# Issue order at the start, five accumulator banks in the output projection, and moved weight tiles in a two-layer attention kernel

## The chip, the cores and the metric

The kernel runs on one core of a Trainium2 chip (trn2). The metric is the device time of one execution in microseconds (us), lower is better; the time given for a kernel is the median of its runs. The core has five engines that work side by side and are tied together by semaphores: TensorE (PE, matmul), VectorE (DVE), ScalarE (ACT), GpSimd (POOL) and SyncE (SP, which here only issues transfers).

## The reference

Two layers work on a stream x of 1024 tokens by 1024 features, with 256 memory tokens beside it. All is float32.

```
layer 0:  u = rms_norm(x) * g ; p = u @ w_in      (7168 columns)
          8 heads of differential attention (two softmax maps each, position bias, q and k normalised)
          a gated causal convolution of width 3 over 512 channels
          4 heads of attention to the memory tokens
          h = x + concat(each branch * silu(its gate)) @ w_out
layer 1:  the same frame, with 12 heads of "forgetting" attention (a cumulative
          log-sigmoid bias per head) and 4 heads of attention to the memory tokens
out = h
```

## The kernel before

**Precision.** A float32 matmul is made from float32r parts: every operand is split into a high part (a ScalarE copy, L128) and the rest (a subtraction on VectorE or GpSimd, L129), and each product is three matmuls: high by high, high by low, low by high. The helper is `split` (L125). Weights come through raw buffers in SBUF (tag "raw", four of them) and are split into `wqh`/`wql` (eight tiles each, tags of the pool `pw`) or, for gate and convolution columns, into `wfh`/`wfl`.

**Start.** `run` (L810) opens two pools for layer 0, `p1_0` and then `pw_0`, takes the norm weights `gb` and goes over eight blocks of 128 tokens. For each it loads x (tag "E1", three buffers) on the SP queue, squares it on ScalarE (L135), gets the reciprocal root on GpSimd (L120, L122), scales on VectorE (L137), transposes on TensorE (L146) and splits the result into `u`, the moving or stationary operand of all projections. Ahead of the third block it asks for the weights of the first head's q, k and v columns: `unit_weights` (L167) makes eight tiles of 384 columns, each from three transfers of 64 KB, with the low parts alternately on VectorE and GpSimd. Behind the blocks come `params` (L64: small transfers of per-feature gains, some with a small product on VectorE) and `lam_setup` (L478: a transfer, three VectorE steps and an exponential on ScalarE). Then `diff_head(0)` runs the unit: `token_unit` (L187), eight blocks of 24 matmuls with 384 columns. While `boot` is set the unit takes accumulator banks from the tags "d" and "s" in turn. After the first head's gate columns, the function `first` (L830) does the memory branch of both layers: `mem_norm` and `mem_kv`.

**PSUM.** Of eight banks, tag "d" has three (projections), "s" two (attention scores), "t" two (transposes) and "o" one (attention outputs).

**Output projection.** `out_proj` (L763) opens a pool `p2` when the layer's `p1` and `pw` are closed; the pools share addresses, and a tile waits for those that it overlies (`reuse_waits="tile"`). In `p2` lie 32 tiles `wo` of 2 KB per partition for the second half of the output columns (first the 16 high parts, then the 16 low parts), `gb2` and four tiles `hb`. The first half of the columns goes over token blocks in pairs: `out_blocks` (L737) takes one "d" bank for each block, and over four groups of four chunks loads y back (ACT queue), splits it into `yh`/`yl` (three buffers each) and runs 12 matmuls per block and group. When a pair is done, VectorE adds the residual in `hb` (L782) and frees the banks. The second half goes block by block and, in layer 0, normalises each finished block for layer 1 (L805).

**Layer 1.** `run` opens `p1_1` and then `pw_1` where `p2_0` was. `fox_head(0)` (L669) runs a unit of 396 columns (12 more for the forget gates), with the low weight parts all on GpSimd.

**Order.** The kernel's text does not fix the order of the queues. The framework plans it with a simulated clock: among the instructions that are ready it takes the one with the highest priority, which is the place in the text unless a block raises it (`high_priority` by 4000 or 8000 places). Each engine then works through its queue strictly in that order.

Of the kernel before, what the change touches and what calls it, by code (L numbers as in the profile page):

```python
# [7 lines left out]
F32 = mybir.dt.float32  # L8
F32R = mybir.dt.float32r
# [6 lines left out]
P = 128  # L16
T = 1024
D = 1024
# [8 lines left out]
PRIO_EVAC, PRIO_ATT = 8000, 4000  # L27
# [6 lines left out]
class Trunk:  # L34
# [26 lines left out]
        self.attb, self.gorder = 3, (3, 2, 1, 0)  # L61
        self.wq_n, self.e1b, self.ptb = 384, 3, 2

    def params(self):  # L64
        nc, io = self.nc, self.io

        def col(name, src, n, reps=1):
            t = self.const.tile([P, 1], F32, name=name)
            for r in range(reps):
                nc.sync.dma_start(out=t[r * n:(r + 1) * n, :], in_=src.rearrange("a n -> n a"))  # L70
            return t

        def prod(name, a, b, s):
            t = self.const.tile([P, 1], F32, name=name)
            nc.vector.tensor_tensor(out=t, in0=a, in1=b, op=ALU.mult)
            nc.vector.tensor_scalar(out=t, in0=t, scalar1=s, scalar2=None, op0=ALU.mult)
            return t

        self.g_a = prod("g_a", col("aq", io["e_a_q_norm_g"], 64, 2), col("ak", io["e_a_k_norm_g"], 64, 2), 64.0 ** -0.5)
        self.g_c = prod("g_c", col("cq", io["o_c_q_norm_g"], P), col("ck", io["o_c_k_norm_g"], P), float(P) ** -0.5)  # L80
        self.g_x = [
            prod("g_x0", col("xq0", io["e_x_q_norm_g"], P), col("xk0", io["e_x_k_norm_g"], P), float(P) ** -0.5),
            prod("g_x1", col("xq1", io["o_x_q_norm_g"], P), col("xk1", io["o_x_k_norm_g"], P), float(P) ** -0.5),
        ]
        og = col("og", io["e_a_out_norm_g"], P)
        self.g_o = self.const.tile([P, 1], F32, name="g_o")
        nc.vector.tensor_scalar(out=self.g_o, in0=og, scalar1=0.5 * (1.0 - LAM_INIT), scalar2=None, op0=ALU.mult)

        self.lam = self.const.tile([P, 1], F32, name="lam")
        self.cw = self.const.tile([P, 4, 3], F32, name="cw")  # L90
        for k in range(3):
            nc.sync.dma_start(out=self.cw[:, :, k], in_=io["e_b_conv_w"][0, k].rearrange("(g p) -> p g", p=P))
        self.cb = self.const.tile([P, 4], F32, name="cb")
        nc.sync.dma_start(out=self.cb, in_=io["e_b_conv_b"][0].rearrange("(g p) -> p g", p=P))
        self.fb = self.const.tile([P, 12], F32, name="fb")
        nc.sync.dma_start(out=self.fb, in_=io["o_c_forget_b"].broadcast_to([P, 12]))
# [357 lines left out]
    def qkv_unit(self, w, cols, ng, gs, g, extra=None, pairs=False, weights=None):  # L454
        nc = self.nc
        qh, ql, kh, kl, vh, vl = self.att_tiles("qh", "ql", "kh", "kl", "vh", "vl")
        kd, kz = self.att_tiles("kd", "kz") if pairs else (None, None)
        qns = []

        def post(tb, ps):  # L460
            raw = self.evac(ps, 384 if extra is None else 396)
            qns.append(self.qk_norm(raw, ng, gs))
            vs = slice(tb % 4 * P, (tb % 4 + 1) * P)
            self.split(vh[tb // 4][:, vs], vl[tb // 4][:, vs], raw[:, 256:384], nc.gpsimd)
            if extra is not None:
                extra[1](tb, raw)
            if tb % 2:
                if pairs:
                    self.later(DEFER, lambda: self.qk_transpose_pairs(qns[tb - 1:tb + 1], (qh, ql), (kh, kd, kl, kz), g, (tb - 1) * P))
                else:  # L470
                    self.later(DEFER, lambda: self.qk_transpose(qns[tb - 1:tb + 1], [(qh, ql, g), (kh, kl, None)], (tb - 1) * P))
        if weights is None:
            weights = self.unit_weights(w, [(c, P) for c in cols] + ([] if extra is None else [extra[0]]))
        self.token_unit(weights, self.u_lhs(0), self.u_lhs(1), NB, post)
        return (qh, ql), (kh, kd, kl, kz) if pairs else (kh, kl), *[(lambda kb, v=v: v[kb // 4][:, kb % 4 * P:(kb % 4 + 1) * P]) for v in (vh, vl)]

# [260 lines left out]
    def out_blocks(self, layer, tbs, tiles, fetch=None):  # L737

        nc = self.nc
        pss = [self.bank("pd", "d") for _ in tbs]  # L740
        for j in range(4):
            if fetch is not None:
                fetch(range(4 * j, 4 * j + 4))
            for tb, ps in zip(tbs, pss):
                ts = slice(tb * P, (tb + 1) * P)
                yr = self.pk.tile([P, 4, P], F32, name="yr2", tag="yr", bufs=4)
                nc.scalar.dma_start(out=yr, in_=self.y_dr[layer][tb // 2][j][tb % 2])
                if layer == 0 and j < 2:
                    rn = self.pa.tile([P, 4, P], F32, name="rn", tag="hs", bufs=3)
                    nc.scalar.dma_start(out=rn, in_=self.on_dr[j][tb].unsqueeze(0).broadcast_to([P, 4, P]))  # L750
                    nc.gpsimd.tensor_tensor(out=yr, in0=yr, in1=rn, op=ALU.mult)
                yh = self.pa.tile([P, 4, P], F32R, name="yh2", tag="wfh", bufs=3)
                yl = self.pa.tile([P, 4, P], F32R, name="yl2", tag="wfl", bufs=3)
                self.split(yh, yl, yr, nc.vector)
                for i in range(4):
                    c = 4 * j + i
                    h, l = tiles(0, c), tiles(1, c)
                    nc.tensor.matmul(ps, lhsT=yh[:, i, :], rhs=h, start=(c == 0), stop=False)  # L758
                    nc.tensor.matmul(ps, lhsT=yh[:, i, :], rhs=l, start=False, stop=False)  # L759
                    self.last_mm = nc.tensor.matmul(ps, lhsT=yl[:, i, :], rhs=h, start=False, stop=(c == 15))  # L760
        return pss

    def out_proj(self, layer, w, res, dst, g_next):  # L763
        nc, tc = self.nc, self.tc
        with tc.tile_pool(name=f"p2_{layer}", bufs=1, reuse_waits="tile") as p2:
# [2 lines left out]
            u, early = self.u, self.early  # L768
            ne = len(early[0])
            w0 = lambda part, c: early[part][c] if c < ne else u[part][(c - ne) // 8][:, (c - ne) % 8, :]  # L770
            ws = [[p2.tile([P, 512], F32R, name=f"wo{p}_{c}") for c in range(16)] for p in range(2)]
            w1 = lambda part, c: ws[part][c]

            gb = p2.tile([P, D], F32, name="gb2")
            hbs = [p2.tile([P, D], F32, name=f"hb{i}") for i in range(4)]
# [34 lines left out]
    def run(self, out):  # L810
        nc, tc, io = self.nc, self.tc, self.io
        mem = io["mem"][0]
        with tc.tile_pool(name="p1_0", bufs=1, reuse_waits="tile") as self.p1, tc.tile_pool(name="pw_0", bufs=1, reuse_waits="tile") as self.pw:
            gb = self.pk.tile([P, T], F32, name="gb", tag="bias", bufs=1)
            self.new_u()
            w, weights = io["e_w_in"][0], None
            for tb in range(NB):
                if tb == 2:
                    weights = self.unit_weights(w, [(c, P) for c in self.diff_cols(0)], (nc.vector, nc.gpsimd))
                with tc.high_priority(PRIO_EVAC):  # L820
                    xn = self.p1.tile([P, T], F32, name="xn", tag="E2", bufs=2)
                    x = self.p1.tile([P, T], F32, name="x", tag="E1", bufs=self.e1b)
                    nc.sync.dma_start(out=x[:, :D], in_=io["x"][0, tb * P:(tb + 1) * P, :])
                    if tb == 0:
                        nc.sync.dma_start(out=gb, in_=io["e_norm_g"].broadcast_to([P, D]))
                    self.norm_block(x[:, :D], gb, xn[:, :D], *self.u_dst(tb))
            self.params()
            self.lam_setup()

            def first():  # L830
                kv = self.mem_kv(0, self.mem_norm(0, mem, io["e_mem_norm_g"]), io["e_w_mem_kv"][0])
                for _ in range(2):
                    next(kv)
                kv1 = self.mem_kv(1, self.mem_norm(1, mem, io["o_mem_norm_g"]), io["o_w_mem_kv"][0])
                for _ in (*kv, *kv1):
                    pass
                self.bias = self.pk.tile([P, T], F32, name="abias", tag="bias", bufs=1)
                nc.gpsimd.iota(self.bias, pattern=[[1, T]], base=-(NB - 1) * P, channel_multiplier=-1, allow_small_or_imprecise_dtypes=True)
                nc.gpsimd.affine_select(out=self.bias, in_=self.bias, pattern=[[-1, T]], compare_op=ALU.is_ge, fill=NEG,
                                        base=(NB - 1) * P, channel_multiplier=1)  # L840
# [5 lines left out]
            for pr in range(2):  # L846
                self.x_pair(0, pr, w, 6144, 6656, io["e_w_out"][0])
        self.out_proj(0, io["e_w_out"][0], io["x"][0], self.h_dr, io["o_norm_g"])
        with tc.tile_pool(name="p1_1", bufs=1, reuse_waits="tile") as self.p1, tc.tile_pool(name="pw_1", bufs=1, reuse_waits="tile") as self.pw:
            self.wq_n, self.e1b, self.ptb = 396, 3, 3  # L850
            w = io["o_w_in"][0]
            self.cqn = self.p1.tile([P, NB, 12], F32, name="cqn")
# [36 lines left out]
```

## Time and profile before

| what | value |
|---|---|
| median of three runs | 2222.51 us (2221.56 to 2222.58) |
| the profiled execution | 2226.73 us, its span 2224.9 us |
| TensorE busy | 2177.0 us, 98% of the span |
| VectorE, ScalarE, GpSimd busy | 1251.2, 1057.3 and 1025.4 us |
| moved by transfers | 183.05 MB, mean 82 GB/s |

Times in the rows are microseconds from the start of the span, unless ns is marked. PE is TensorE, PEld its weight load, DVE VectorE, ACT ScalarE, POOL GpSimd, SPq and ACTq the queues that issue transfers. In a timeline row the bracket says how long the engine was idle before the instruction and what ended that. PEclk is the granted clock of TensorE as a share of 2.4 GHz; 0.50 is 1.2 GHz. Matmuls overlap, so the distance from start to start, not the duration, is what one costs.

### The profile page before, as it was taken

To read this page: it belongs to the slowest core of one execution; us is meant where nothing else is said; L and a number is where in the kernel's file an instruction comes from. 1 tells how busy PE (TensorE), PEld (TensorE's weight loads), DVE (VectorE), ACT (ScalarE), POOL (GpSimd) and SP (SyncE) were. 2 spreads that over 40 slices of the span, in tenths; PEclk is the share of its full clock that TensorE was granted. 3 is DMA by queue.
4 is the path that set the end of the run, shared out by engine and by line. 5 is a ranking of instruction groups with operands and counts; after the bars stand their busy time and mean duration, and the time that the engine had idled before them with its cause. 6 is when DMAs were issued, how large, how long until landed. Compare 5 with 4: busy or idle time off the path is not lost.

```text
span 2224.9 us, 35832 instructions
## 1 busy us (share of the span) xinstructions
PE 2177.0 (98%) x12528; PEld 1975.1 (89%) x12528; DVE 1251.2 (56%) x2860; ACT 1057.3 (48%) x2503; POOL 1025.4 (46%) x1356
## 2 busy tenths in 40 slices
PE   7999999999999999999989999999999999999999
PEld 6889889899898899777879999999999999998787
DVE  5646656665665667653525555555555555666432
ACT  5655465464554555432334444444444444554321
POOL 4565555555555453342335555544555555431200
PEclk9999999999999999999999999999999999999999
DMA  5350210201202112486522222211222221123643
GB/s 164 123 158 23 65 52 19 72 28 52 62 26 59 36 53 89 127 269 190 182 60 49 58 58 58 58 35 47 46 55 67 58 62 43 47 70 121 220 130 103
DMA packets 222108, 183.05 MB, mean 82 GB/s; under 512 B 24636, under 2 KB 179420, under 8 KB 221928
## 3 DMA queue, kind: packets, MB, share of 16 engines
q1 hardware_dynamic: 198888, 138.82, 21.8%
q10 hardware_dynamic: 23040, 41.95, 6.2%
q8 instruction: 98, 1.61, 0.3%
q14 instruction: 82, 0.67, 0.1%
HBM read 153.32 MB, written 27.38 MB: 81 GB/s over the span
## 4 chain that ended last, share of the span: by engine, by line
PE 91%; DMA 4%; DVE 1%; ACT 1%; POOL 1%; issue 1%; SPq 1%; ACTq 0%; POOLq 0%; DVEq 0%
PE pd L199 11%; PE pd L200 11%; PE pd L198 11%; PE pss L391 8%; PE pd L232 7%; PE pd L231 7%; PE pd L233 7%; PE pd L758 5%; PE pd L760 5%; PE pd L759 5%; PE pt L425 4%; PE po L439 2%; PE po L440 2%; PE po L438 2%; PE pt L280 1%
## 5 line engine op out<-in xcount | busy, mean ns | idle before, releaser
L198 PE MATMUL pd<-wqh,u 128*128 128x384 f32 (+2 forms) x1536 | 515.7, 337 | 3.3 <-ACT wqh L128 2.4
L199 PE MATMUL pd<-wql,u 128*128 128x384 f32 (+2 forms) x1536 | 514.3, 335 | 1.8 <-POOL wql L129 1.8
L200 PE MATMUL pd<-wqh,u 128*128 128x384 f32 (+2 forms) x1536 | 513.7, 335 | 0.0
L198 PEld LDWEIGHTS pd<-wqh,u 128*128 128x128 f32 x1536 | 291.3, 190 | 7.7 <-ACT wqh L128 3.0
L199 PEld LDWEIGHTS pd<-wql,u 128*128 128x128 f32 x1536 | 291.6, 190 | 6.8 <-POOL wql L129 2.2
L200 PEld LDWEIGHTS pd<-wqh,u 128*128 128x128 f32 x1536 | 291.2, 190 | 4.4
L231 PE MATMUL pd<-u,wfh 128*128 128x512 f32 x704 | 278.8, 397 | 0.0
L232 PE MATMUL pd<-u,wfl 128*128 128x512 f32 x704 | 278.8, 396 | 0.0
L233 PE MATMUL pd<-u,wfh 128*128 128x512 f32 x704 | 278.4, 396 | 0.0
L129 POOL TENSOR_TENSOR wql<-raw,wqh 128x384 fp32r<-128x384 f32 (+2 forms) x220 | 216.4, 995 | 79.5 <-ACT wqh L128 74.5
L271 DVE TENSOR_TENSOR qr<-qr,rs_r 128x256 f32<-128x256 f32 x200 | 139.4, 697 | 100.7 <-POOL rs_r L122 98.6
L128 ACT ACTIVATE yh<-yr 128x512 fp32r<-128x512 f32 x128 | 80.7, 631 | 224.1 <-PE pd L759 147.1
L128 ACT ACTIVATE pth<-pt 128x512 fp32r<-128x512 f32 (+1 forms) x232 | 121.9, 555 | 133.5 <-PE pt L425 125.9
L129 DVE TENSOR_TENSOR yl<-yr,yh 128x512 fp32r<-128x512 f32 x128 | 100.3, 784 | 150.0 <-ACT yh L128 141.8
L122 POOL TENSOR_TENSOR rs_r<-rs_v,neghalf 128x2 f32<-128x2 f32 (+2 forms) x220 | 177.7, 809 | 14.0
L695 POOL TENSOR_TENSOR fbias<-ck,cqn 128x896 f32<-128x896 f32 (+3 forms) x96 | 110.3, 1149 | 156.0 <-DVE mx L408 123.8
L128 ACT ACTIVATE wqh<-raw 128x384 fp32r<-128x384 f32 (+2 forms) x256 | 118.3, 480 | 121.0 <-DMA raw<-in_e_w_in_dram 60.8
L129 POOL TENSOR_TENSOR wfl<-rawf,wfh 128x512 fp32r<-128x512 f32 x88 | 120.8, 1374 | 108.9 <-ACT wfh L128 106.6
L129 DVE TENSOR_TENSOR ptl<-pt,pth 128x512 fp32r<-128x512 f32 (+1 forms) x232 | 143.8, 640 | 44.2 <-ACT pth L128 42.1
L129 POOL TENSOR_TENSOR vl<-qr,vh 128x128 fp32r<-128x128 f32 x160 | 81.1, 513 | 174.5 <-ACT vh L128 167.6
L233 PEld LDWEIGHTS pd<-u,wfh 128*128 128x128 f32 x704 | 132.8, 189 | 27.5 <-issue 1.1
L232 PEld LDWEIGHTS pd<-u,wfl 128*128 128x128 f32 x704 | 132.8, 189 | 26.5 <-issue 1.4
(277 smaller groups left out, 4978.5 us busy)
## 6 DMA issues: line engine op xcount, KB each, us to landing
yr<-y_dr ACTq DMA_DIRECT2D x128, 256.0 KB
raw<-in_o_w_in_dram SPq DMA_DIRECT2D x288, 64.0 KB
rawf<-in_e_w_in_dram SPq DMA_DIRECT2D x56, 256.0 KB
y_dr<-y SPq DMA_DIRECT2D x112, 128.0 KB
raw<-in_e_w_in_dram SPq DMA_DIRECT2D x192, 64.0 KB
wraw<-in_e_w_out_dram SPq DMA_DIRECT2D x32, 256.0 KB
rn<-on_dr ACTq DMA_DIRECT2D x32, 256.0 KB
rawf<-in_o_w_in_dram SPq DMA_DIRECT2D x32, 256.0 KB
```

The costliest lines, as they stand in the source:

```text
L122: nc.gpsimd.tensor_tensor(out=r[:, :n], in0=v[:, :n], in1=self.neghalf[:, :n], op=ALU.pow)
L128: nc.scalar.activation(out=hi, in_=src, func=AF.Copy)
L129: lo_eng.tensor_tensor(out=lo, in0=src, in1=f32(hi), op=ALU.subtract)
L198: nc.tensor.matmul(ps[:, :n], lhsT=ah(k), rhs=h, start=(k == 0), stop=False)
L199: nc.tensor.matmul(ps[:, :n], lhsT=ah(k), rhs=l, start=False, stop=False)
L200: mm = nc.tensor.matmul(ps[:, :n], lhsT=al(k), rhs=h, start=False, stop=(k == KC - 1))
L231: nc.tensor.matmul(ps, lhsT=h, rhs=uh[:, k, :], start=(k == 0), stop=False)
L232: nc.tensor.matmul(ps, lhsT=l, rhs=uh[:, k, :], start=False, stop=False)
L233: nc.tensor.matmul(ps, lhsT=h, rhs=ul[:, k, :], start=False, stop=(k == KC - 1))
L271: nc.vector.tensor_tensor(out=v, in0=v, in1=r.unsqueeze(2).broadcast_to([P, ng, gs]), op=ALU.mult)
L391: nc.tensor.matmul(ps, lhsT=q[qb // 4][rows, qs], rhs=k[c0 // 512][rows, ks], start=(i == 0), stop=(i == n - 1))
L758: nc.tensor.matmul(ps, lhsT=yh[:, i, :], rhs=h, start=(c == 0), stop=False)
```

## The change

- `out_blocks` takes an "s" bank for the second block of each pair but the first, so that the first half of an output projection has five banks.
- The `wo` tiles are made in the order of chunks, high and low part side by side, not all high parts first.
- `run` loads x of block 0 and the norm weights ahead of all else, and asks for the first unit's weights ahead of block 1, at the raised priority.
- `params` makes only `g_a` ahead of the first unit; the rest of it and `lam_setup` move into `first`, behind the first head's gate.
- In layer 1 `pw_1` is opened before `p1_1`, so the weight tiles lie at the addresses of the first `wo` tiles.
- The first fox head's low weight parts alternate between VectorE and GpSimd.

```diff
-    def params(self):
+    def params(self, first):
...
-        self.g_a = prod("g_a", col("aq", io["e_a_q_norm_g"], 64, 2), col("ak", io["e_a_k_norm_g"], 64, 2), 64.0 ** -0.5)
+        if first:
+            self.g_a = prod("g_a", col("aq", io["e_a_q_norm_g"], 64, 2), col("ak", io["e_a_k_norm_g"], 64, 2), 64.0 ** -0.5)
+            return
...
-            weights = self.unit_weights(w, [(c, P) for c in cols] + ([] if extra is None else [extra[0]]))
+            weights = self.unit_weights(w, [(c, P) for c in cols] + ([] if extra is None else [extra[0]]), None if extra is None else (nc.vector, nc.gpsimd))
...
-        pss = [self.bank("pd", "d") for _ in tbs]
+        pss = [self.bank("pd", "s" if i % 2 and tb > 1 else "d") for i, tb in enumerate(tbs)]
...
-            ws = [[p2.tile([P, 512], F32R, name=f"wo{p}_{c}") for c in range(16)] for p in range(2)]
-            w1 = lambda part, c: ws[part][c]
+            ws = [[p2.tile([P, 512], F32R, name=f"wo{p}_{c}") for p in range(2)] for c in range(16)]
+            w1 = lambda part, c: ws[c][part]
...
+            with tc.high_priority(PRIO_EVAC + 100):
+                x0 = self.p1.tile([P, T], F32, name="x", tag="E1", bufs=self.e1b)
+                nc.sync.dma_start(out=x0, in_=io["x"][0, :P, :])
+                nc.sync.dma_start(out=gb, in_=io["e_norm_g"].broadcast_to([P, D]))
             for tb in range(NB):
-                if tb == 2:
-                    weights = self.unit_weights(w, [(c, P) for c in self.diff_cols(0)], (nc.vector, nc.gpsimd))
+                if tb == 1:
+                    with tc.high_priority(PRIO_EVAC):
+                        weights = self.unit_weights(w, [(c, P) for c in self.diff_cols(0)], (nc.vector, nc.gpsimd))
                 with tc.high_priority(PRIO_EVAC):
                     xn = self.p1.tile([P, T], F32, name="xn", tag="E2", bufs=2)
-                    x = self.p1.tile([P, T], F32, name="x", tag="E1", bufs=self.e1b)
-                    nc.sync.dma_start(out=x[:, :D], in_=io["x"][0, tb * P:(tb + 1) * P, :])
-                    if tb == 0:
-                        nc.sync.dma_start(out=gb, in_=io["e_norm_g"].broadcast_to([P, D]))
+                    x = x0 if tb == 0 else self.p1.tile([P, T], F32, name="x", tag="E1", bufs=self.e1b)
+                    if tb:
+                        nc.sync.dma_start(out=x, in_=io["x"][0, tb * P:(tb + 1) * P, :])
                     self.norm_block(x[:, :D], gb, xn[:, :D], *self.u_dst(tb))
-            self.params()
-            self.lam_setup()
+            self.params(True)

             def first():
+                self.params(False)
+                self.lam_setup()
                 kv = self.mem_kv(0, self.mem_norm(0, mem, io["e_mem_norm_g"]), io["e_w_mem_kv"][0])
...
-        with tc.tile_pool(name="p1_1", bufs=1, reuse_waits="tile") as self.p1, tc.tile_pool(name="pw_1", bufs=1, reuse_waits="tile") as self.pw:
+        with tc.tile_pool(name="pw_1", bufs=1, reuse_waits="tile") as self.pw, tc.tile_pool(name="p1_1", bufs=1, reuse_waits="tile") as self.p1:
```

## Rows read from the trace of the kernel before

**Rows 1.** The page's first part: the span, then each engine's busy time.

```profile
span 2224.9 us, 35832 instructions
PE 2177.0 (98%) x12528; PEld 1975.1 (89%) x12528; DVE 1251.2 (56%) x2860; ACT 1057.3 (48%) x2503; POOL 1025.4 (46%) x1356
```

**Rows 2.** TensorE's waits, whole span: total us, times, longest.

```profile
PE pt L146 <- DVE xn L137: 9.6, 1, 9.6
PE pd L758 <- DVE hb L782: 6.9, 2, 5.0
PE pt L146 <- DVE u L129: 5.5, 2, 4.3
```

**Rows 3.** Stretches: length, busy PE, PEld, DVE, ACT, POOL; clock, transfer share, GB/s.

```profile
0.00:63.30 63.30, 47.10 (x266) 44.83 (x266) 36.61 (x65) 38.16 (x83) 30.32 (x58) 0.95 0.49 144
...
38.90:45.70 6.80, 4.70 (x17) 4.20 (x18) 5.67 (x7) 4.22 (x10) 6.31 (x11) 0.52 0.55 182
...
1134.60:1141.40 6.80, 5.33 (x17) 5.32 (x18) 1.17 (x2) 2.17 (x5) 5.02 (x5) 0.52 0.35 71
...
2069.80:2076.60 6.80, 5.15 (x12) 4.04 (x13) 2.47 (x4) 1.86 (x4) 1.17 (x1) 0.51 0.90 301
...
1200.00:2000.00 800.00, 800.00 (x5008) 760.96 (x5007) 454.29 (x1159) 375.40 (x914) 410.98 (x610) 1.00 0.21 53
```

**Rows 4.** Timeline of the start: start, us, engine, line, operation, idle before.

```profile
0.72 0.87 SPq L823 DMA_DIRECT2D x<-in_x_dram  x2
...
4.60 1.06 ACT L135 ACTIVATE xn<-x 128x1024 f32<-128x1024 f32 x1 [2.60 <-DMA x<-in_x_dram]
...
8.29 2.48 DVE L137 SCALAR_TENSOR_TENSOR xn<-x,rs_r,gb 128x1024 f32<-128x1024 f32 x2 [3.65 <-DMA gb<-in_e_norm_g_dram]
...
13.43 5.30 SPq L177 DMA_DIRECT2D raw<-in_e_w_in_dram  x9
...
30.57 0.63 DVE L75 TENSOR_TENSOR g_x<-xq,xk 128x1 f32<-128x1 f32 x2 [2.92 <-DMA xk<-in_e_x_k_norm_g_dram]
...
39.78 1.11 PE L146 MATMUL pt<-ident,xn 128*128 128x128 f32 x4 [4.27 <-DVE u L129]
...
62.90 0.34 PE L199 MATMUL pd<-wql,u 128*128 128x384 f32 x1
63.08 0.34 PE L200 MATMUL pd<-wqh,u 128*128 128x384 f32 x1
```

**Rows 5.** Timeline of the output projection of layer 0.

```profile
959.40 1.90 SPq L780 DMA_DIRECT2D hb<-in_x_dram  x4
...
964.99 0.47 PE L758 MATMUL pd<-kd,yh 128*128 128x512 f32 x1 [1.87 <-DVE hb L782]
```

**Rows 6.** Timeline of the seam between the layers.

```profile
1133.58 1.28 DVE L137 SCALAR_TENSOR_TENSOR xn<-hb,rs_r,gb 128x1024 f32<-128x1024 f32 x1
1134.94 1.38 ACT L128 ACTIVATE wqh<-raw 128x396 fp32r<-128x396 f32 x3 [1.58 <-DVE xn L137]
...
1136.07 0.70 PE L199 MATMUL pd<-wql,u 128*128 128x396 f32 x1 [1.85 <-POOL wql L129]
...
1154.83 0.45 PE L280 MATMUL pt<-ident,qr 128*128 128x128 f32 x1 [2.85 <-DVE qr L271]
```

**Rows 7.** Timeline of the output projection of layer 1.

```profile
2023.79 0.28 PE L391 MATMUL pss<-vh,kl 128*128 128x256 f32 x1
...
2065.14 3.67 SPq L780 DMA_DIRECT2D hb<-h_dr  x4
...
2070.71 0.69 DVE L782 TENSOR_TENSOR hb<-pd,hb 128x512 f32<-128x512 f32 x1 [2.33 <-DMA hb<-h_dr]
...
2071.45 0.80 PE L758 MATMUL pd<-kd,yh 128*128 128x512 f32 x1 [4.98 <-DVE hb L782]
```

**Rows 8.** Groups of VectorE's instructions, first 70 us: busy us, mean ns, idle.

```profile
L129 DVE TENSOR_TENSOR wql<-raw,wqh 128x384 fp32r<-128x384 f32 x4 | 2.3, 569 | 2.1 <-ACT wqh L128 2.1
```

**Rows 9.** One line's instructions (L129): ns shortest/median/longest, first and last start.

```profile
L129 DVE TENSOR_TENSOR wo<-wraw,wo x16: 677/1307/1785, 960.7 to 2092.8; 128x512 fp32r<-128x512 f32 x16
```

## The prediction

> **What bounds the kernel.** I read the page's busy times first. TensorE is busy for 2177.0 of 2224.9 us of span [rows 1], so only 48 us are idle. A busy TensorE can still run at half clock, so the second view is the table of stretches. From 1200 to 2000 us TensorE is busy in all of it, at granted clock 1.00 [rows 3]: nothing that other engines do there can shorten it. What can be gained lies in a few holes and in the stretches of 1.2 instead of 2.4 GHz behind them. The list of TensorE's waits names the holes [rows 2]: 9.6 us for the first normalised block, 5.5 us for transposed blocks, 6.9 us (two waits) for output-projection banks. The timeline adds two between the layers [rows 6]. Behind the holes lie stretches of 6.8 us with the clock at 0.51 to 0.52: around 39.78, 1134 and 2069 us [rows 3]. Each costs its busy time times what the clock lacks: 4.70 x 0.48 = 2.3, 5.33 x 0.48 = 2.6, 5.15 x 0.49 = 2.5 us. The reader should see that the change touches exactly these places: the start, both output projections, and the seam between the layers.
>
> **Output projection, layer 1.** out_blocks runs token blocks in pairs on three "d" banks. The first pair holds two until hb is added (L782). Row by row [rows 7]: hb is loaded from 2065.14, the add waits 2.33 us for it and starts at 2070.71, and TensorE, which has run out of banks, waits 4.98 us, until 2071.45. Why so late: hb lies in memory of the pools just closed, and SP takes its loads behind the last attention store. The edit gives the odd block of each later pair an "s" bank. The last score matmul, the only other user of "s", starts at 2023.79 [rows 7], over 40 us earlier, so that bank is free. The 4.98 us go, and with no hole the low stretch behind it should go too: 4.98 + 2.5 = 7.5 us. What is late next: VectorE is strictly in order, so the add that waits for hb holds back the yl splits queued behind it. TensorE then lives on blocks already split: three buffers of 12 matmuls, each 0.18 us x 512/384 = 0.24 us long [rows 4], so 8.6 us, more than the 5.0 to be covered. If only one of the three is ready, 2.9 us are covered and the low clock stays. Bounds 2.9 to 7.5; I take 7.5, the upper end, because a hole that is gone leaves no reason for the low clock.
>
> **Output projection, layer 0.** The same hole is 1.87 us at 964.99 [rows 5], hb being issued at 959.40. It goes by the same bank. But behind it come loads of y, row norms and weights; if those set the pace, the gain is given back. Bounds 0 to 1.9, I take 1.5, near the upper end, as these loads are issued when TensorE frees buffers and so move forward with it.
>
> **Order of the wo tiles.** It changes addresses only. No instruction is added. In layer 0 and layer 1 the tiles are written after the attention has ended, as hb is [rows 5, 7]. By itself it is worth nothing; it lets the next edit overlay pieces that are read early.
>
> **Pool order at the seam.** Now the first fox head's weight tiles overlie hb and the norm weights, so three of the four first wqh splits wait 1.58 us for the last norm (1133.58, 1.28 us), and TensorE waits 1.85 us for wql, until 1136.07 [rows 6]. With pw first they overlie wo tiles of low chunk numbers, read early in the last block: that run-time wait goes. But the order of the queues is written by a planner, and the three splits, though free, stand behind the last norm in it; I assume the planner still opens a pool only when the old one's last user has been placed. The first wql split moves from GpSimd to VectorE (even chunks), where it stands behind that norm: 1133.58 + 1.28 = 1134.86, and 0.57 us for a split of 384 columns [rows 8] gives 1135.4 against 1136.07: 0.6 us. The later hole of 2.85 us at 1154.83 [rows 6], where three blocks finish together and their norm is late, shrinks by about as much as the later weights come earlier: GpSimd's row of four splits is halved, about 1 us. I take 1.6. Bounds: nothing, and all of 1.85 + 2.85 + 2.6 for the clock = 7.3.
>
> Here a rule speaks against the edit. Splits on VectorE with both inputs in SBUF take 0.68 to 1.79 us for 512 columns [rows 9], a spread that splits of one shape should not have. The Trainium skill (GPSIMD Engine Reference, Specifications) says that GpSimd's SBUF interfaces are shared with VectorE and that VectorE instructions with two SBUF inputs contend. The trace agrees, as the 1.79 shows. By it the first split could take 1.79 x 396/512 = 1.4 us, ending at 1136.2: the seam's first hole stays as it is, and my sum falls by 0.8 us.
>
> **The start.** The unit's last matmul starts at 63.08; TensorE is busy in 47.10 of the first 63.30 us [rows 3, 4]. Three things move.
> (a) Block 0 and the norm weights go first. VectorE waits 3.65 us for gb, whose load stands behind two x loads [rows 4]. x of block 0 is there at 4.60 and gb at 8.29, so x of block 1 and gb, 512 KB each, share 3.7 us: taking one of them away saves half, 1.8. First transposes at 7.8 instead of 9.6.
> (b) The 24 weight loads go ahead of x of block 1. SP takes 5.30 us for nine [rows 4], 0.59 each. Four raw buffers hold 12 loads: if SP is then held by buffers, x of block 1 goes out at 1.6 + 12 x 0.59 = 8.7 us; if not, behind all 24, at 15.8. From issue to first use a block needs 3.9 us to land (0.72 to 4.60) and, as block 0 shows, 5.0 more to the transposes at 9.63 [rows 2, 4] (the wait for gb in it stands for the copies that follow): 9 together. Block 1 then starts at 17.7 or 24.8. A block costs TensorE 24 matmuls at 0.18 and eight transposes of a third of that: 4.8 us; seven make 33.6. The unit ends at 51.3, or at 58.4 plus 2.3 for a low stretch behind the hole, 60.7. Now: 63.3.
> (c) All parameters but g_a, and lambda, move behind the unit. Each is a tiny load on SP plus a small VectorE or ScalarE step which blocks its queue until the load lands: 2.92 us on VectorE at 30.57 [rows 4], which makes the blocks' norms late; the hole of 4.27 us at 39.78 follows. Behind the unit the same loads (13 on SP, 13 x 0.59 = 7.7 us) stand ahead of the memory branch's. They depend on nothing, so the planner may put them into the same empty SP slots and the stall comes back: up to 4.27 + the 1.2 rest of the 5.5 us [rows 2] = 5.5 us lost.
> Ends: 12.0 gained to 60.7 + 5.5 = 66.2, 2.9 lost. The middle of the two loading orders is a gain of 7.3; half the 5.5 comes off, as nothing tells whether the planner repeats the stall. I take 4.5.
>
> **Sum.** 4.5 + 1.5 + 1.6 + 7.5 = 15.1 us. The profiled execution took 2226.7 us (span 2224.9), 4.2 above the median of the runs, 2222.5; I take the sum off both: 2211.6 profiled, 2207.4 as median. By the rule of the Trainium skill it would be 2208.2.
>
> **Rivals.**
> 1. *Full cure*: x of block 1 slips in behind four raw tiles and the parameter stall goes. Start 12.0; the rest 10.6: 2199.9. For it: the buffers' number. Against it: SP's 0.59 us per load is slower than the splits that free them.
> 2. *Starved start*: all 24 weights first and the stall returns. Start -2.9, rest 10.6: 7.7 gained, 2214.8. For it: the priorities put the weights ahead of block 1.
> 3. *Moved wait*: freed from the bank, TensorE soon stands before yl, because VectorE stands before hb. Layer 1 gives 2.9, layer 0 nothing, the seam nothing: 4.5 + 2.9 = 7.4, 2215.1. For it: the add at 2070.71 and in-order VectorE.
> 4. *Slower*: the planner writes all queues anew from simulated times. The middle is free of idle time [rows 3], so it can only get worse. A hole as at 964.99 (1.87) with half of a low stretch (1.2), in 12 of the 20 attention heads, costs 12 x 3.1 = 37 us: 2245. It decides from five such heads on, 15.5 us, which eat up the sum. Against it: the middle has buffers ready and TensorE waits for nothing there now.
>
> **Numbers.** Forecast 0.55, full cure 0.14, starved 0.13, moved wait 0.12, slower 0.06. What a measurement of this kernel can tell from no change is 0.2%, 4.4 us. Faster by more (under 2218.1): the forecast and the full cure, nearly all of the starved and the moved case, less what lies near their lower ends: 0.87. Within 0.2%: 0.08. Slower: 0.05. The range leaves out the best tenth of the full cure and the slower cases: 2196 to 2219.
>
> **What would show it.** Layer 1: no wait on hb at L758, clock 1.00 through 2060 to 2080. Layer 0: none near 965, and no longer wait for yh or yl after it. Seam: wqh splits without waiting for xn, wql at 1135.4 on this clock, a shorter wait at L280. Start: unit's end before 63; x of block 1 issued at 9 or at 16 us; no VectorE wait for xk inside the unit. I am wrong if the middle shows holes, or if the unit ends after 63.

## The result: 2208.4 us, and the profile after

The changed kernel takes 2208.38 us (median of 4 runs, 2208.13 to 2213.06) against 2222.03 us before (4 runs beside it, 2221.24 to 2222.58): ratio 0.9944, 95% interval 0.9927 to 0.9961. Run again beside other runs of the kernel before (e5_again below) it took 2208.97 against 2220.86 us, ratio 0.9950 (0.9936 to 0.9964). So 12 to 14 us are gained, where 15.1 were forecast. Its profiled execution took 2208.35 us. The page's first part, which answers to [rows 1]:

```profile
span 2206.6 us, 35844 instructions
...
PE 2170.4 (98%) x12528; PEld 1971.3 (89%) x12528; DVE 1250.3 (57%) x2864; ACT 1057.1 (48%) x2503; POOL 1021.0 (46%) x1352
```

The same matmuls, 6.6 us less busy time and 11.7 us less idle time.

TensorE's waits over the whole span (total us, times, longest), which answer to [rows 2]:

```profile
PE pt L148 <- DVE xn L139: 7.9, 1, 7.9
PE pd L200 <- ACT wqh L130: 4.3, 3, 2.2
PE pt L282 <- DVE qr L273: 4.1, 3, 2.9
...
PE pd L201 <- DVE wql L131: 2.3, 1, 2.3
PE pt L148 <- DVE u L131: 2.1, 3, 1.0
PE pd L760 <- ACT yh L130: 2.1, 3, 0.9
PE pd L762 <- DVE yl L131: 1.3, 2, 0.8
```

(Line numbers behind line 80 are two higher: L758, L782, L129 are now L760, L784, L131.) The wait for output-projection banks (6.9 us) has left the list; the first block costs 7.9 instead of 9.6 us, the transposed blocks 2.1 instead of 5.5. The waits of the seam have stayed or grown: before, wqh cost 4.3 us as well (2.19 of them at the seam), wql 1.8 and qr 3.1.

Stretches (length; busy PE, PEld, DVE, ACT, POOL; clock, transfer share, GB/s), which answer to [rows 3]:

```profile
0.00:57.30 57.30, 45.56 (x264) 43.45 (x265) 34.67 (x62) 37.74 (x82) 28.82 (x58) 1.00 0.54 157
...
1122.40:1129.20 6.80, 5.54 (x17) 5.52 (x18) 2.25 (x4) 0.92 (x2) 2.58 (x2) 0.50 0.38 75
1200.00:2000.00 800.00, 799.09 (x5011) 759.31 (x5010) 454.94 (x1164) 377.38 (x921) 403.56 (x602) 1.00 0.21 53
2040.00:2080.00 40.00, 40.00 (x184) 32.82 (x183) 16.56 (x26) 13.96 (x25) 7.05 (x6) 1.00 0.69 221
```

The first unit now fits into 57.3 us at full clock; the middle is as it was, but for one hole of 0.9 us; the start of the layer-1 projection has no idle time and no low clock. The reader should see the third gain missing: the seam still has its 6.8 us at half clock, now from 1122.4 us on, and the table of waits says why.

The two traces can't simply be subtracted: the profiled execution of before, 2226.73 us, lies 4.7 us above the median of the runs beside it. So I cut each profiled execution at the same events (first scores, first and last matmul of each output projection, end) and compared kernels with and without an edit over all of them. "Scores" are the score matmuls, the projections L758 to L760.

| stretch (us) | edit absent | mean | edit present | mean | gain |
|---|---|---|---|---|---|
| start to first scores, all three start edits | 130.9 to 134.2 (4 profiles) | 132.5 | 125.5 to 130.0 (6) | 127.3 | 5.2 |
| layer-0 projection, "s" bank | 193.7 to 197.3 (5) | 195.4 | 193.8 to 197.1 (8) | 194.9 | 0.5 |
| seam: last layer-0 projection matmul to layer 1's first scores | 61.2 to 63.6 (4) | 62.8 | 63.3 to 64.6 (5) | 64.2 | -1.3 |
| layer-1 projection, first to last matmul, "s" bank | 188.0 to 189.8 (5) | 189.0 | 182.1 to 182.8 (8) | 182.4 | 6.6 |

Together 11.0 us. The terms predicted were 4.5, 1.5, 1.6 and 7.5. The stretches between these agree within about 3 us in all profiles. The layer-0 row mixes in a second edit: of the kernels without the "s" bank, the three with the old order of the wo tiles take 195.4 to 197.3 us, the two with the new order (e3_seam, e10_pool_alone) 193.7 and 194.3; e1_bank, with the bank and the old order, takes 194.8. The order of the wo tiles was never run alone, so whether it is worth something there, where the prediction gave it nothing, stays open.

### The profile page after: what moved, and what is told of

Read it like the earlier page. It is cut to its first block, busy times and chain, and to the rows that moved or that the text cites. A ratio compares the mean times of both kernels' runs of the same rounds, so it can differ in the third digit from the quotient of the medians.

```text
span 2206.6 us, 35844 instructions
## 1 busy us (share of the span) xinstructions
PE 2170.4 (98%) x12528; PEld 1971.3 (89%) x12528; DVE 1250.3 (57%) x2864; ACT 1057.1 (48%) x2503; POOL 1021.0 (46%) x1352
## 4 chain that ended last, share of the span: by engine, by line
PE 92%; DMA 3%; DVE 2%; POOL 1%; issue 1%; ACT 1%; SPq 0%; ACTq 0%; POOLq 0%; DVEq 0%
PE pd L201 12%; PE pd L202 12%; PE pd L200 12%; PE pss L393 8%; PE pd L234 7%; PE pd L233 7%; PE pd L235 7%; PE pd L762 5%; PE pd L760 5%; PE pd L761 5%; PE pt L427 4%; PE po L441 2%; PE po L442 2%; PE po L440 2%; PE pt L282 1%
## 5 line engine op out<-in xcount | busy, mean ns | idle before, releaser
L131 POOL TENSOR_TENSOR wql<-raw,wqh 128x384 fp32r<-128x384 f32 (+2 forms) x216 | 213.9, 1002 | 85.1 <-ACT wqh L130 81.3
L131 DVE TENSOR_TENSOR yl<-yr,yh 128x512 fp32r<-128x512 f32 x128 | 100.1, 782 | 145.9 <-ACT yh L130 127.5
L131 POOL TENSOR_TENSOR wfl<-rawf,wfh 128x512 fp32r<-128x512 f32 x88 | 121.1, 1378 | 107.0 <-ACT wfh L130 106.3
L131 DVE TENSOR_TENSOR ptl<-pt,pth 128x512 fp32r<-128x512 f32 (+1 forms) x232 | 143.7, 639 | 43.8 <-ACT pth L130 41.7
L131 POOL TENSOR_TENSOR vl<-qr,vh 128x128 fp32r<-128x128 f32 x160 | 80.2, 508 | 171.0 <-ACT vh L130 163.9
L235 PEld LDWEIGHTS pd<-u,wfh 128*128 128x128 f32 x704 | 132.3, 188 | 27.3 <-issue 1.1
L234 PEld LDWEIGHTS pd<-u,wfl 128*128 128x128 f32 x704 | 132.5, 188 | 26.3 <-issue 1.4
```

The lines of the kernel that those rows point to most:

```text
L131: lo_eng.tensor_tensor(out=lo, in0=src, in1=f32(hi), op=ALU.subtract)
L234: nc.tensor.matmul(ps, lhsT=l, rhs=uh[:, k, :], start=False, stop=False)
L235: nc.tensor.matmul(ps, lhsT=h, rhs=ul[:, k, :], start=False, stop=(k == KC - 1))
```

## The experiments

All medians stand beside runs of the kernel before on the same chip: 2221.85 us (e1 to e4), 2220.86 (e5 to e8), 2220.45 (e9 to e12). Single executions of one kernel lie up to 6 us either side of their median.

### The change cut into three: e1_bank, e2_start, e3_seam

e1_bank is the kernel before with one line changed:

```
-        pss = [self.bank("pd", "d") for _ in tbs]
+        pss = [self.bank("pd", "s" if i % 2 and tb > 1 else "d") for i, tb in enumerate(tbs)]
```

> The kernel before with the bank edit alone (odd blocks of the later pairs on an "s" bank). My sum: layer 0 gives 1.5 us and layer 1 gives 7.5 us, 9.0 in all, so 2213.0 us against a median of 2222.0; layer 1 without a wait on hb at L758. Rival, the moved wait: TensorE soon stands before yl because VectorE stands before hb, layer 1 gives 2.9 and layer 0 nothing: 2219.1 us. Second rival, the two traces read side by side (events matched: 3.6 us in layer 0, 6 to 7 in layer 1): 2211.9 us.

Measured 2215.50 us (7 runs), ratio 0.9971 (0.9960 to 0.9982): 6.4 us gained. TensorE no longer waits at all in the layer-1 projection; in layer 0 the wait for hb is gone, and this stands in its place:

```profile
963.71 0.50 PE L760 MATMUL pd<-kd,yl 128*128 128x512 f32 x1 [1.69 <-DVE yl L129]
```

The moved wait is real in layer 0 and absent in layer 1: the edit's 6.4 us are the 6.6 of the last row of the table. Every other kernel with the bank waits for yl at this place too, for 0.46 us (the changed kernel) to 2.18 us (e5_again, the same kernel).

e2_start is the kernel before with the edits of run() and params() alone.

```
+            with tc.high_priority(PRIO_EVAC + 100):
+                x0 = ...
-                if tb == 2:
+                if tb == 1:
...
-            self.params()
-            self.lam_setup()
+            self.params(True)
             def first():
+                self.params(False)
+                self.lam_setup()
```

> The kernel before with the edits of the start alone (block 0 and the norm weights first, weight loads ahead of block 1, parameters behind the first unit). My sum: 4.5 us, 2217.5 us. Rival, the two traces read side by side (8.4 us gained by the end of the memory branch): 2213.6 us. Rival, part of that was only the profiled execution of before, which lay 4.2 us above its median: then the gain of medians is between these, and the trace of before at its median would show a shorter start.

Measured 2217.31 us (11 runs), ratio 0.9976 (0.9967 to 0.9985): 4.5 us, as my sum has it. The 8.4 us of the two traces came in part from which execution of before was profiled.

e3_seam is the kernel before with pool order, order of the wo tiles and the split on VectorE.

```
-            ws = [[p2.tile([P, 512], F32R, name=f"wo{p}_{c}") for c in range(16)] for p in range(2)]
+            ws = [[p2.tile([P, 512], F32R, name=f"wo{p}_{c}") for p in range(2)] for c in range(16)]
...
-        with tc.tile_pool(name="p1_1", ...) as self.p1, tc.tile_pool(name="pw_1", ...) as self.pw:
+        with tc.tile_pool(name="pw_1", ...) as self.pw, tc.tile_pool(name="p1_1", ...) as self.p1:
...
-            weights = self.unit_weights(w, [...])
+            weights = self.unit_weights(w, [...], None if extra is None else (nc.vector, nc.gpsimd))
```

> The kernel before with the edits of the seam alone (pool order, order of the wo tiles, low parts of the first fox head's weights on VectorE and GpSimd in turn). My sum: 1.6 us, 2220.4 us. Rival, the trace of the changed kernel: the wait for wql there grew from 1.85 to 2.29 us and the hole at the transposes of qr stayed (2.85 and 2.86 us), so nothing or a loss of about 0.5 us: 2222.0 to 2222.5 us. Rival, full cure: 7.3 us, 2214.7 us.

Measured 2222.31 us (11 runs), ratio 1.0003 (0.9994 to 1.0012): nothing gained. The three parts add to 6.4 + 4.5 - 0.5 = 10.4 us, against 11.9 to 13.7 for the whole, inside the intervals.

### The seam: e4_wql, e10_pool_alone, e8_fox5, e12_banks

e4_wql is the changed kernel without the split on VectorE; e10_pool_alone is e3_seam without it.

```
-            weights = self.unit_weights(w, [...], None if extra is None else (nc.vector, nc.gpsimd))
+            weights = self.unit_weights(w, [...])
```

> The changed kernel with the first fox head's low parts all on GpSimd again. If the split on VectorE costs at the seam because it stands behind the last norm (and may contend), taking it away leaves the new pool order to work by itself: the hole before wql, 2.29 us, goes, with some of the low clock behind it, up to 2.3 + 2.6 = 4.9 us faster than the changed kernel, 2203.5 us. By my own step, in which VectorE's half saves 0.6 us at wql and 1 us at the later transposes, it is 1.6 us slower: 2210.0 us.

> The kernel before with pool order and order of the wo tiles alone, low parts on GpSimd as before (e3_seam without the split on VectorE). If the profile of e4_wql is right (from the last output block to the first scores 58.5 us against 63.5 before): 5 us faster than before and than e3_seam, 2216.4 us. If its times are (2210.0 us, no better than the changed kernel): 2221.4 us.

e4_wql: 2210.02 us (5 runs), 0.9945 (0.9929 to 0.9961). e10_pool_alone: 2219.39 us (11 runs), 0.9992 (0.9983 to 1.0001). By the times neither is told apart from its partner. What happens is read from the traces. The changed kernel at the seam, in the order of its rows:

```profile
1119.98 1.80 ACT L130 ACTIVATE wqh<-raw 128x396 fp32r<-128x396 f32 x4
1120.56 0.81 PE L200 MATMUL pd<-wqh,u 128*128 128x396 f32 x3 [2.19 <-ACT wqh L130]
1120.73 1.28 DVE L139 SCALAR_TENSOR_TENSOR xn<-hb,rs_r,gb 128x1024 f32<-128x1024 f32 x1
1121.01 3.98 POOL L131 TENSOR_TENSOR wql<-raw,wqh 128x396 fp32r<-128x396 f32 x2 [0.45 <-ACT wqh L130]
1122.27 0.91 DVE L658 MEMSET fg_on<- 12x1024 f32 x1 [0.27 <-DVE xn L139]
1123.11 0.97 DVE L131 TENSOR_TENSOR wql<-raw,wqh 128x396 fp32r<-128x396 f32 x2
...
1123.66 0.70 PE L201 MATMUL pd<-wql,u 128*128 128x396 f32 x1 [2.29 <-DVE wql L131]
...
1142.66 0.30 PE L282 MATMUL pt<-ident,qr 128*128 128x128 f32 x1 [2.86 <-DVE qr L273]
```

And e4_wql:

```profile
1126.51 0.81 PE L200 MATMUL pd<-wqh,u 128*128 128x396 f32 x3 [2.19 <-ACT wqh L130]
1126.54 5.99 POOL L131 TENSOR_TENSOR wql<-raw,wqh 128x396 fp32r<-128x396 f32 x5
1126.68 1.97 DVE L139 SCALAR_TENSOR_TENSOR xn<-hb,rs_r,gb 128x1024 f32<-128x1024 f32 x1
1127.63 0.45 PE L201 MATMUL pd<-wql,u 128*128 128x396 f32 x1 [0.31 <-POOL wql L131]
...
1144.44 0.30 PE L282 MATMUL pt<-ident,qr 128*128 128x128 f32 x1 [2.86 <-DVE qr L273]
```

The pool order does what it should: the four wqh splits start in one piece, without waiting for the last norm [rows 6]. In the changed kernel the first low part then stands on VectorE behind that norm and behind a memset for the forget gates. On GpSimd it is ready at once: the wait for wql is 0.31 us in e4_wql and in e10_pool_alone, 1.75 to 2.30 us in every profile with the split on VectorE and 1.50 to 1.85 in those with the old pool order. By these rows the split gives back what the pool order gained: the first wql matmul starts 4.58 us behind the last projection matmul in e4_wql and e10_pool_alone, 6.12 us with the old pool order, 6.57 us with the split. The whole seam takes 58.5 us in e4_wql and 62.4 in e10_pool_alone, against 64.2 with the split and 62.8 without any seam edit. So the 1.5 us that the pool order gains at wql are hardly seen at the end of the seam in e10_pool_alone; e4_wql, whose profiled execution lay 3.1 us under its median, differs by a granted clock of 1.00 in all of it.

The memset is no work of the new order. It stood behind the norm in the trace of before too, where GpSimd did four low parts in the time that two take in the changed kernel (3.98 us at 1121.01):

```profile
1134.99 3.99 POOL L129 TENSOR_TENSOR wql<-raw,wqh 128x396 fp32r<-128x396 f32 x4 [1.58 <-DVE xn L137]
1135.00 0.91 DVE L656 MEMSET fg_on<- 12x1024 f32 x1
```

The 2.19 us before the first wqh are in all fourteen profiles. In the changed kernel ScalarE works without a gap from 1117.97 us on the last block's square and the copies of u, and the first wqh stands behind them at 1119.98; no edit here touches that.

The hole of 2.86 us at the transposes of qr keeps its size in all of these. Three token blocks run side by side on three "d" banks, end together, and then everything waits for their norms. e8_fox5 gives that unit five banks, on top of e4_wql:

```
+        self.boot = h == 0
         q, k, vh, vl = self.qkv_unit(...)
+        self.boot = False
```

> The changed kernel with the first fox head's low parts on GpSimd (as in e4_wql) and its token blocks alternating between "d" and "s" banks, as in the first unit. Theory: the hole of 2.86 us at the transposes of qr is a bank wait in the main, three blocks holding all "d" banks until their norms are done; with five banks the fourth block fills it, and the low clock behind it goes too (1.5 us): 4.4 us faster than e4_wql, 2205.6 us. Rival: TensorE's order has the transposes ahead of the fourth block's matmuls all the same: no change against e4_wql, 2210.0 us.

Measured 2203.37 us (5 runs), 0.9923 (0.9909 to 0.9937); the changed kernel on the same chip 2208.97, 0.9950 (0.9936 to 0.9964). Its median is below those of e4_wql and of the changed kernel, but the intervals still overlap a little. The 40 us behind the last projection matmul (columns as above) in the changed kernel, e4_wql, e12_banks (below) and e8_fox5:

```profile
1117.10:1157.10 40.00, 32.65 (x165) 31.57 (x164) 13.48 (x29) 14.45 (x34) 16.62 (x23) 0.87 0.26 60
...
1123.05:1163.05 40.00, 34.57 (x197) 33.16 (x196) 14.46 (x29) 15.94 (x38) 20.98 (x30) 1.00 0.27 60
...
1120.00:1160.00 40.00, 36.06 (x195) 34.97 (x194) 15.17 (x33) 16.05 (x38) 18.45 (x26) 0.91 0.26 60
...
1122.40:1162.40 40.00, 37.67 (x208) 36.75 (x207) 14.47 (x31) 17.96 (x44) 22.03 (x33) 0.96 0.26 60
```

In e8_fox5 TensorE does 208 instead of 165 matmuls in 40 us, the clock is 0.96 instead of 0.87, and neither wql nor qr is waited for; only the 2.19 us before the first wqh are left.

e12_banks is e8_fox5 with the split on VectorE again.

> e8_fox5 with the first fox head's low parts on VectorE and GpSimd in turn, that is the changed kernel with the five banks at the seam and nothing else. If the banks alone cure the seam: 2203.4 us, as e8_fox5. If the first split still stands behind the last norm and a memset on VectorE (2.29 us before wql) and brings the low clock: 2 to 4 us slower than e8_fox5, 2206.5 us.

Measured 2205.91 us (5 runs), 0.9928 (0.9916 to 0.9941), between the two. Its wait for wql is back, 1.75 us, and the seam takes 58.1 us against 55.8. So the banks alone clear the hole at qr, and the split on VectorE still costs its wait. Which of the two edits is worth more is not shown: in one profiled execution each, either alone brings the seam from 63.3 to 64.2 us (changed kernel, two profiles) down to about 58 (58.1 and 58.5), both together to 55.8; by the times neither alone is clear of the noise.

### The start: e5_again, e6_params, e7_weights, e9_params_alone

e5_again is the changed kernel itself.

> The changed kernel once more, beside the same kernel before as the three that follow. If its first median holds: 2208.4 us. If that rested on few executions and the parts simply add (6.4 for the banks, 4.5 for the start, -0.5 for the seam): 2211.6 us.

2208.97 us (6 runs): the first median holds. e6_params puts parameters and lambda back ahead of the unit, e7_weights asks for the weights at the third block without priority, and e9_params_alone does the parameter edit alone, on the kernel before:

```
 e6_params, against the changed kernel
             self.params(True)
+            self.params(False)
+            self.lam_setup()
             def first():
-                self.params(False)
-                self.lam_setup()
 e7_weights, against the changed kernel
-                if tb == 1:
-                    with tc.high_priority(PRIO_EVAC):
+                if tb == 2:
```

> The changed kernel with all parameters and lambda asked for ahead of the first unit again. By my step (c) half of the 5.5 us of the old stall comes back: 2.8 us slower than the changed kernel, 2211.2 us, with VectorE waiting for a parameter inside the unit and the unit's end some 3 us later. Rival: the planner puts these loads into the same empty places in either case (in the changed kernel VectorE does them from 24.7 to 30.4 us, inside the unit), so nothing changes: 2208.4 us, unit's last matmul at 57 us.

> The changed kernel with the first unit's weights asked for at the third token block, without the priority, as before. By my step (b), which was the larger part of the start, 7.3 less 1.8: 5.5 us slower than the changed kernel, 2213.9 us. Rival: in the changed kernel SP took x of blocks 1 and 2 at 2.10 us, behind a single weight load, so the weights were not put ahead at all, and the gain of the start is that of the first block: within 1 us, 2208.4 to 2209.4 us.

> The kernel before with the parameters and lambda behind the first unit, and nothing else. If they carry the start, as e6_params says (5.6 us lost when they are put back): 5 us faster than before, 2216.5 us, without the 4.27 us hole in the first unit. By my step (c), half of 5.5: 2.8 us, 2218.6 us. If their move only pays once the weights are early: 2221.4 us.

| kernel | median, us | ratio to before | unit's last matmul | first scores |
|---|---|---|---|---|
| start edits absent (4 profiles) | | | 61.5 to 63.1 | 130.9 to 134.2 |
| all but the parameters: e6_params | 2214.54 | 0.9972 (0.9963 to 0.9981) | 63.3 | 132.3 |
| parameters alone: e9_params_alone | 2219.91 | 0.9992 (0.9982 to 1.0002) | 61.1 | 132.6 |
| all but the weights: e7_weights | 2211.51 | 0.9957 (0.9942 to 0.9971) | 58.9 | 129.3 |
| all: changed kernel, e5_again | 2208.97 | 0.9950 (0.9936 to 0.9964) | 57.3, 57.5 | 125.5, 126.6 |

Putting the parameters back costs 5.6 us, twice my step and nearly the whole gain of the start; moving them alone gives nothing that can be measured. Both kernels have a hole at the place of the old one, of 2.38 and 2.30 us instead of 4.27. e6_params:

```profile
31.67 0.43 SPq L483 DMA_DIRECT2D lp<-in_e_a_lambda_dram  x1
32.14 0.98 SPq L224 DMA_DIRECT2D rawf<-in_e_w_in_dram  x2
...
35.80 0.29 DVE L485 TENSOR_TENSOR lpm<-lp 128x128 f32<-128x128 f32 x1 [0.98 <-DMA lp<-in_e_a_lambda_dram]
36.72 0.63 ACT L130 ACTIVATE wfh<-rawf 128x512 fp32r<-128x512 f32 x1 [2.40 <-DMA rawf<-in_e_w_in_dram]
...
40.87 0.66 PE L148 MATMUL pt<-ident,xn 128*128 128x128 f32 x4 [2.38 <-DVE u L131]
```

e9_params_alone:

```profile
27.50 1.40 SPq L70 DMA_DIRECT2D ck<-in_o_c_k_norm_g_dram  x1
...
31.33 0.18 DVE L75 TENSOR_TENSOR g_c<-cq,ck 128x1 f32<-128x1 f32 x1 [3.43 <-DMA ck<-in_o_c_k_norm_g_dram]
...
38.91 0.65 PE L148 MATMUL pt<-ident,xn 128*128 128x128 f32 x4 [2.30 <-DVE u L131]
```

In the first, the parameter loads on SP push the gate's weights back to 32.14 us, and ScalarE, in strict order, stands 2.40 us before them with the norms of the last blocks behind. In the second, the gate's weights are early (issued at 23.46 us), but the parameters still go out among the x loads, and VectorE stands 3.43 us before one of them. By these rows a wait on either engine is enough for a hole. In the changed kernel the parameters are still computed inside the unit, but the waits are short or early: 1.91 and 0.22 us on VectorE before 27.1 us, 1.60 us on ScalarE before the gate's weights at 25.82 instead of 36.72 us. What is left of the hole there is 0.31 and 0.78 us.

```profile
21.64 1.08 SPq L224 DMA_DIRECT2D rawf<-in_e_w_in_dram  x2
22.77 0.49 SPq L70 DMA_DIRECT2D cq<-in_o_c_q_norm_g_dram  x1
...
24.68 0.16 DVE L75 TENSOR_TENSOR g_a<-aq,ak 128x1 f32<-128x1 f32 x1 [1.91 <-DMA ak<-in_e_a_k_norm_g_dram]
...
27.05 0.96 DVE L75 TENSOR_TENSOR g_c<-cq,ck 128x1 f32<-128x1 f32 x1 [0.22 <-DMA ck<-in_o_c_k_norm_g_dram]
```

The weights' order is worth 2.5 us by the medians (2211.51 less 2208.97), with overlapping intervals; half of the 5.5 I had put on it, and more than the rival allowed. It was not settled further.

### One step on: e11_oneload

```
-            for c0, cn in groups:
-                nc.sync.dma_start(out=raw[:, :, o:o + cn], in_=w[...])
+            if per == 1 and ...:   # three groups equally far apart
+                nc.sync.dma_start(out=raw[:, 0, :3 * cn].rearrange("p (g c) -> p g c", g=3), in_=src)
```

> e8_fox5 with the three column groups of a weight chunk in one load instead of three. Theory: at the start and at the seam the weights come at SP's pace (four issues of some 0.47 us for each raw tile at the seam, and in the first unit three), so a quarter to a third as many issues brings the first unit's weights and the x blocks earlier: 1 to 3 us faster than e8_fox5, 2201 us. Rival: x, norms and the copies of transposed blocks set the pace of the first unit, not the weights: no change, 2203.4 us.

Measured 2201.46 us (4 runs), 0.9907 (0.9893 to 0.9920), the fastest of all, 19 us under the kernel before. But the theory is not borne out: the unit's last matmul is at 57.7 us, no earlier than in e8_fox5 (57.4), and the seam takes 57.6 us against 55.8. What is shorter in its profile than in that of e8_fox5 is the layer-0 projection (192.7 against 197.1 us) and the way from layer 1's first scores to the end (1023.2 against 1025.9, but 1023.6 in e4_wql too), neither of which the edit explains. That it beats the kernel before and the changed one is measured; that it beats e8_fox5 is not.

## Why the prediction came out

**The time was right, the sum somewhat too large.** 2207.4 us was forecast, 2208.4 and 2209.0 measured; the sum of 15.1 us stands against 13.7 and 11.9 by times, and 11.0 by stretches. That it came so near is in part luck: one term had the wrong sign, and the size of the start was the middle between two loading orders of which neither came about. Term by term, against the table of stretches:

- **Layer-1 projection: right, 6.6 instead of 7.5 us.** No wait on hb, 40.00 busy of 40.00 us, clock 1.00. As predicted, VectorE still waits for hb (1.44 us at 2062.24), and TensorE lives on blocks already split. The size was off in part since the profiled execution of before had the longest hole of five: 4.98 us against 3.92 to 4.73 in the others.
- **Layer-0 projection: 0.5 instead of 1.5 us, and not told apart from nothing.** The failed sentence is that the loads "move forward with it". What is late next is yl or yh, as rival 3 has it: in the changed kernel 0.46, 0.68, 0.95 and 0.83 us from 955 to 978, in e1_bank 1.69 and 0.22 us in that stretch. Rival 3's mechanism is true in layer 0 and false in layer 1, where e1_bank has no idle time. The wait for hb alone does not part them, as it is longer in layer 1. The order of VectorE's queue differs, here in e1_bank:

```profile
958.58 3.07 DVE L129 TENSOR_TENSOR wo<-wraw,wo 128x512 fp32r<-128x512 f32 x2 [1.74 <-ACT wo L128]
962.37 0.69 DVE L782 TENSOR_TENSOR hb<-pd,hb 128x512 f32<-128x512 f32 x1 [0.72 <-DMA hb<-in_x_dram]
962.98 0.68 DVE L129 TENSOR_TENSOR yl<-yr,yh 128x512 fp32r<-128x512 f32 x1
...
2065.91 0.69 DVE L129 TENSOR_TENSOR yl<-yr,yh 128x512 fp32r<-128x512 f32 x1 [0.71 <-ACT yh L128]
2066.95 1.37 DVE L129 TENSOR_TENSOR wo<-wraw,wo 128x512 fp32r<-128x512 f32 x1 [0.35 <-ACT wo L128]
2069.95 0.69 DVE L782 TENSOR_TENSOR hb<-pd,hb 128x512 f32<-128x512 f32 x1 [1.62 <-DMA hb<-h_dr]
```

  In layer 0 two splits of wo and the add stand ahead of the yl that TensorE needs; in layer 1 a yl goes ahead of one split of wo and the add. No run changed that order, so that it decides is read from the rows and not tried.
- **Pool order: the assumption on the planner failed.** I took it that the wqh splits would still stand behind the last norm. They don't wait for it, and with GpSimd alone wql follows 1.1 us later.
- **Split on VectorE: the wrong sign.** The step priced 1.28 us of norm and 0.57 us of split, and overlooked the memset of 0.91 us that stands between them (at 1135.00 already before); wql came 0.45 us later instead of 0.6 us earlier. It gave 1.6 us for the seam; -1.3 were measured by stretches (e3_seam: -0.5 by times, not told apart from nothing). The other 1 us was to come from GpSimd's row of splits, halved from four to two; two now take 3.98 us where four took 3.99. The hole of 2.85 us at qr kept its size, in e4_wql and e10_pool_alone too, and e8_fox5 and e12_banks show that it hangs on banks.
- **The start: right in size, 5.2 instead of 4.5 us (e2_start: 4.5), by other shares.** Step (a) is as worked out: first transposes at 7.89 us, 7.8 forecast. Step (b) is wrong in its picture: x of block 1 went out neither at 9 nor at 16 us but at 2.10, behind one weight load. Nor did the weights move much: before (first row), eleven of the 24 loads already went out from 2.58 us on, and the last went out by 20.6 us in both kernels.

```profile
2.58 8.70 SPq L177 DMA_DIRECT2D raw<-in_e_w_in_dram  x11
...
0.72 0.39 SPq L821 DMA_DIRECT2D x<-in_x_dram  x1
1.17 0.42 SPq L822 DMA_DIRECT2D gb<-in_e_norm_g_dram  x1
1.64 0.42 SPq L179 DMA_DIRECT2D raw<-in_e_w_in_dram  x1
2.10 0.91 SPq L831 DMA_DIRECT2D x<-in_x_dram  x2
3.05 6.71 SPq L179 DMA_DIRECT2D raw<-in_e_w_in_dram  x8
```

  Step (c) was named, as a stall that may come back, and mis-sized: undoing it costs 5.6 us, while doing it alone gives nothing measurable. So the parts don't add: with (c) alone or all but (c) the first scores start at 132.6 and 132.3 us, as without any start edit (130.9 to 134.2). By the rows above they are waits one behind the other on the same path.
- **The slower rival** did not come: from the first scores to the last all profiles take 792.9 to 795.4 us in layer 0, and 830.1 to 831.9 in layer 1 (without e11_oneload, where the projection starts before the last scores). The one hole of 0.9 us in the middle of layer 1, at qr, is a sign of being wrong that the prediction named; it is too small to count.
- **The rule on shared interfaces: the price fell on the other engine.** The Trainium skill (GPSIMD Engine Reference, Specifications) says that VectorE instructions with two SBUF inputs contend with GpSimd. The rows at the seam agree. VectorE's splits took 495 and 546 ns, where I had allowed 1.4 us; of GpSimd's, the one beside the norm took 1873 ns and the one beside VectorE's two splits 2140, and 1040 and 1051 later without VectorE's. So TensorE's wait for wql came from the queue, not from the contention; what the overlap cost is about a microsecond in each of GpSimd's two splits, and with it the halving above.

## What to carry to other kernels

Work moved onto a less busy engine pays only if it does not land behind something late in that engine's order: look up what will stand ahead of it, and which engine the waiting matmul needs first. Where several token blocks end together and then wait for their norms, look for an idle bank before touching the norms; one line gave 6.4 us in the projections, and two cleared the hole at qr that the pool order and the split had left. Waits in a row on one path must be undone together, and an edit tried alone may look worthless; cut several profiled executions at the same events before subtracting two traces, since one of them can be several microseconds off its median.

## What the hardware showed beyond that

- Executions of one kernel differ by several microseconds without any change: the kernel before gave 2216.1 to 2227.0 us over the three sets of runs. Part of it lies in the holes: in two profiled executions of the changed kernel (the first and e5_again) the wait for yl in layer 0 was 0.46 and 2.18 us.
- Not every hole is followed by the same clock. In the changed kernel, with holes of 2.19 and 2.29 us close together at the seam, the granted clock is 0.50 (1.2 GHz) from 1122.4 to 1129.2 us, and again for 3.4 us behind the hole of 2.86 us. In e4_wql, with holes of 2.19, 0.31 and 2.86 us, it is 1.00 in all the 40 us shown above; in e8_fox5, with the 2.19 us alone, it is 0.50 for 3.4 us (1127.5 to 1130.9).
- Of VectorE's norm and GpSimd's first low part at the seam, the one that starts second is the longer one. In the changed kernel the norm starts 0.28 us ahead and takes 1.28 us, GpSimd's split 1.87; in e4_wql the split starts 0.14 us ahead and takes 1.04 us, the norm 1.97. So it is in e3_seam and e12_banks, and in e8_fox5 and e10_pool_alone.
